# An FFN up-projection computed token-major with moving weight columns, then transposed to channel rows

## The chip, the core and the metric

The kernel runs on one core of a Trainium2 chip. The metric is device time in microseconds of one execution; the kernel before has a median of 1065.43 us over 3 runs (1064.88 to 1066.43).

## What is computed

One decoder layer for 256 tokens of width 2048, in float32. The mixing part (gated convolution, pooling, attention into 256 memory tokens, output projection) stays as it is; the FFN and the final norm follow. With D_FF = 5632:

```python
        h = rmsnorm(x, g_ffn[l])
        u = causal_dwconv(h @ w_up[l], ffn_conv_w[l]) + ffn_conv_b[l]   # 3 taps along the tokens
        gate, val = jnp.split(u, 2, axis=-1)                           # 5632 channels each
        x = x + (jax.nn.silu(gate) * val) @ w_down[l]
    return rmsnorm(x, g_final)
```

## The kernel before

Every float32 operand of a product is split into a high and a low part in the type float32r, and a product is taken as high x high + high x low + low x high. All weights come as one stream of tiles of 1 MB: SyncE's queue loads a tile (`load`, line 118), ScalarE writes its high part (line 129), VectorE the low part by a subtraction (line 130). Loading runs three tiles ahead of use and splitting two; raw, high and low tiles have three buffers each. `next_tile` (line 149) hands out the next tile and issues these steps.

The stages are: memory tokens, the input projection, the mixing work, the output projection (`mm_b`, lines 326 to 344, with transposes of the FFN's input between two of its products, line 719), then the FFN. There the 44 + 44 chunks of 128 gate and value channels go in 22 units of 256 gate and 256 value channels. The units form groups of 8, 7, 5 and 2; the down-projection of a group comes after the next group's first unit, that of the third after all units, and the last one ends the kernel.

An up unit calls `unit_a` for the gates, finishes them, and calls it for the values. `mm_a` (lines 300 to 312) holds weight columns still: for each of 16 chunks k and two chunks of channels, the high weights against the 512 columns of high and low activations of 256 tokens (line 306), then the low weights against the 256 high columns (line 309). The result has channels in rows, in a bank of PSUM whose two halves are still to be added. `up_finish` (line 737) copies one half out on ScalarE (`gather`, line 322), adds the other and multiplies by a row of the tokens' norm factors on VectorE (lines 323, 324). The convolution along the tokens follows: a scaled copy with bias on ScalarE (line 747), two taps on VectorE (line 751), with two zero columns that GpSimd clears as left margin (line 743). Gates go through Silu (line 755); gate times value is split again into the tile `u` (lines 776 to 780).

The down-projection (`down`, lines 782 to 789) goes the other way about: blocks of 128 tokens of `u` stand still and 512 columns of weights move, in two banks by turns. The last group (`down_last`) does the same and then takes 512- or 256-column pieces in one bank (lines 808 to 820).

The first unit differs: its four tiles alternate between gates and values by halves of k, since the second half of the FFN's transposed input is made by 16 transposes after its first tile (line 734). The norm factors are turned into a row by two transposes (`row_of`, line 274).

Tile, the layer that the kernel is written in, puts the instructions of each engine in order between the parts whose order is written out by hand (the head and the last group); it starts from the order of the program and from what is ready. PSUM has 8 banks, handed out one at a time.

Of the kernel before, what the change touches and what calls it, by code (L numbers as in the profile page):

```python
# [15 lines left out]
P = 128  # L16
EPS = 1e-6
HPAD = 6  # buffers for rows with a left margin
WINDOWS = (2, 4, 8, 16)
# Engines whose instructions keep the order of the program in the first and last parts.  # L20
# [4 lines left out]
def kernel(  # L25
# [33 lines left out]
    # Has the activation table loaded before the first data are there.  # L59
    first = cpool.tile([P, 1], F32, name="first")  # L60
    nc.scalar.activation(first, ones[:, 0:1], AF.Copy)
    # Keeps the tensor engine's clock up until the first data are there.
# [8 lines left out]
    # Per-channel vectors, as columns of 128 channels, by transposing rows of 128.  # L71
# [20 lines left out]
    rows = lambda v: v.rearrange("(r c) -> r c", c=P)  # noqa: E731  # L92
# [10 lines left out]
    stream = []  # (source, nk, ncol, pieces)  # L103
# [52 lines left out]
    n_units = NF // 2  # L156
    UNITS = [8, 7, n_units - 17, 2]  # sizes of FFN groups in units of 256 channels
# [20 lines left out]
    # The pool's weights: per pair of groups the three chunks' rows, in the columns of  # L178
    # the output chunks that they reach; wp_at[k] is the first of them.
# [17 lines left out]
    # Chunks of the mix in the order in which they come about.  # L197
# [10 lines left out]
    # A group's down-projection comes after the next group's first unit; that of the  # L208
    # last but one after all units.
    sched = []  # L210
    done = 0
    for gi, (a, n) in enumerate(group_of):
        upto = n_units if gi + 2 >= len(group_of) else a + n + 1
        for u in range(done, upto):
            sched.append(("up", u, [g for g, (b, m) in enumerate(group_of) if b <= u][-1]))
        done = upto
        sched.append(("down", gi, None))
    for what, a, b in sched:
        if what == "up" and a == 0:
            for h in (0, 1):  # L220
                plan_a(w_up, 0, (h,))
                plan_a(w_up, D_UP, (h,))
        elif what == "up":
            plan_a(w_up, a * 256)
            plan_a(w_up, D_UP + a * 256)
        else:
            a0, n = group_of[a]
            for n2 in range(2):
                plan_b(w_down, a0 * 2, n * 2, n2 * 1024, 1024, 2)

# [27 lines left out]
    def rstd_of(ssq, nm):  # L258
        """ssq [P, n] sums of squares -> 1 / sqrt(mean + eps), with a Newton step."""
        n = ssq.shape[1]  # L260
        v = spool.tile([P, n], F32, tag="nv", name=f"v_{nm}")
        r = spool.tile([P, n], F32, tag="nr", name=f"r_{nm}")
        t = spool.tile([P, n], F32, tag="nt", name=f"t_{nm}")
        with tc.high_priority():
            nc.gpsimd.tensor_scalar(v, ssq, 1.0 / D, EPS, op0=ALU.mult, op1=ALU.add)
            nc.scalar.activation(t, v, AF.Sqrt)
            nc.vector.reciprocal(r, t)
            nc.gpsimd.tensor_tensor(t, r, r, op=ALU.mult)
            nc.gpsimd.tensor_tensor(t, t, v, op=ALU.mult)
            nc.gpsimd.tensor_scalar(t, t, -0.5, 1.5, op0=ALU.mult, op1=ALU.add)  # L270
            nc.gpsimd.tensor_tensor(r, r, t, op=ALU.mult)
        return r

    def row_of(r, nm):
        """[P, TB] per-token values -> the same row of S values in every partition."""
        pr = bank(f"prow_{nm}")
        row = cpool.tile([P, S], F32, name=f"row_{nm}")
        with tc.high_priority():
            for tb in range(TB):
                nc.tensor.transpose(  # L280
                    pr[:, tb * P : (tb + 1) * P], r[:, tb : tb + 1].to_broadcast([P, P]), ident
                )
            nc.scalar.activation(row, pr[:, :S], AF.Copy)
        return row
# [35 lines left out]
    def gather(ps, row, o, engine=nc.vector):  # L320
        """(main + corrections) * row -> o [P, S] in SBUF."""
        nc.scalar.activation(o, ps[:, S:], AF.Copy)  # L322
        nc.vector.tensor_tensor(o, ps[:, :S], o, op=ALU.add)
        engine.tensor_tensor(o, o, row, op=ALU.mult)

    def mm_b(ps, wt, actT, ks, tbs, first, last):
        """ps[tb][n] += act[tokens of tb, chunk k] @ w[chunk k, columns of n]."""
# [41 lines left out]
    # The order of the first instructions is that in which the data arrive.  # L369
# [66 lines left out]
    def split_into(o, src, n=S):  # L436
        """float32 [P, n] -> o, its two parts one after the other."""
# [50 lines left out]
    # 1 / (number of tokens averaged) for the first tokens  # L488
# [73 lines left out]
    # The sums run on GpSimd while the next unit's products do; the rest comes after.  # L562
    pending = []

    def pool_sums(ps, i):
# [3 lines left out]
        spans = []  # (first row, last row, group) of this chunk  # L569
# [17 lines left out]
    def pool_means():  # L587
        for i, v, spans, sums in pending:
# [11 lines left out]
            # The convolution's chunks of the mix are free until it comes.  # L600
# [122 lines left out]
    row_2 = None  # L723
    u_tiles = {}

    def up_matmul(u):
        if u:
            return [unit_a(h2T, f"g{u}"), unit_a(h2T, f"v{u}")]
        ps = [[bank(f"pu0_{w}_{mi}") for mi in range(2)] for w in range(2)]
        for h in range(2):  # L730
            for w in range(2):
                mm_a(ps[w], next_tile(), h2T, h * 8, 8, h == 0, h == 1)
                if h == 0 and w == 0:
                    transpose_in(xt, h2T, "g_ffn", range(8, 16), "x2")
        return ps

    def up_finish(ps, u, w):
        """main + corrections, norm, convolution and bias of one half of a unit."""
        outs = []
        for mi in range(2):  # L740
            m = w * NF + u * 2 + mi
            hp = spool.tile([P, S + 2], F32, tag="hpad", name=f"h_{u}_{w}_{mi}", bufs=HPAD)
            nc.gpsimd.memset(hp[:, :2], 0.0)
            gather(ps[mi], row_2, hp[:, 2:])
            t = spool.tile([P, S], F32, tag="w1k", name=f"t_{u}_{w}_{mi}", bufs=6)
            cw = [cvec("ffn_conv_w", j * 2 * NF + m) for j in range(3)]
            nc.scalar.activation(  # L747
                t, hp[:, 2:], AF.Identity, bias=cvec("ffn_conv_b", m), scale=cw[2]
            )
            for s in (1, 0):  # L750
                nc.vector.scalar_tensor_tensor(  # L751
                    t, hp[:, s : s + S], cw[s], t, op0=ALU.mult, op1=ALU.add
# [4 lines left out]
        return outs  # L757

    def up(u, gi):
        nonlocal row_2  # L760
        if gi not in u_tiles:
            u_tiles[gi] = apool.tile([P, 16, 2 * S], F32R, tag="act", name=f"u_{gi}")
        ut = u_tiles[gi]
        base = group_of[gi][0]
        if u == 0:
            ps_g, ps_v = up_matmul(0)
            row_2 = row_of(rstd_sum(ssq4, "x2"), "x2")
            gates = up_finish(ps_g, u, 0)
        else:
            ps_g = unit_a(h2T, f"g{u}")  # L770
            gates = up_finish(ps_g, u, 0)
            ps_v = unit_a(h2T, f"v{u}")
        vals = up_finish(ps_v, u, 1)
        for mi in range(2):
            c = (u - base) * 2 + mi
            nc.vector.tensor_tensor(gates[mi], gates[mi], vals[mi], op=ALU.mult)
            nc.scalar.activation(ut[:, c, :S], gates[mi], AF.Copy)
            nc.vector.tensor_tensor(
                ut[:, c, S:], gates[mi], ut[:, c, :S].bitcast(F32), op=ALU.subtract
            )  # L780

    def down(gi):
        ut = u_tiles[gi]
        nk = group_of[gi][1] * 2
        for n2 in range(2):
            ps = [[bank(f"pd_{gi}_{n2}_{tb}_{n}") for n in range(2)] for tb in range(TB)]
            for i in range(nk // 2):
                mm_b(ps, next_tile(), ut, (2 * i, 2 * i + 1), range(TB), i == 0, i == nk // 2 - 1)
            add_in(ps, n2 * 2, range(TB), f"d{gi}")

    # The last group goes by token blocks and column pieces, each followed by its share
    # of the final norm, so that little is left after the last product.
    def down_last(gi):
        ut = u_tiles[gi]
        nk = group_of[gi][1] * 2
        gfin = wpool.tile([P, D], F32, tag="raw", name="gfin")
        nc.sync.dma_start(gfin, g_final[None, :].to_broadcast([P, D]))
        nc.scalar.activation(gfin, gfin, AF.Copy, scale=-0.5)  # goes with -2 / sqrt
# [28 lines left out]
        def partial(tb):  # L827
            """The mean square + eps, but for the last piece."""
# [4 lines left out]
        def rstd_last(tb):  # L833
            """-2 / sqrt(mean square + eps), with a Newton step."""
# [20 lines left out]
        with tc.manual_schedule(engines=IN_ORDER):  # L855
# [3 lines left out]
            for tb in range(TB):  # L859
                for p in range(2):  # L860
                    add(ps[tb][p], tb, p)
                    square(tb, p)
                    if tb == 0 and p == 0:
                        # has the square root's table loaded
# [23 lines left out]
    for what, a, b in sched:  # L888
        if what == "up":
            up(a, b)  # L890
# [35 lines left out]
```

## Time and profile before

| | |
|---|---|
| median of 3 runs | 1065.43 us (1064.88 to 1066.43) |
| span of the profiled execution | 1064.7 us |
| TensorE products busy | 1054.7 us (99%), 5632 |
| weight loads on TensorE busy | 907.2 us (85%) |
| VectorE busy | 703.6 us (66%) |
| ScalarE busy | 529.0 us (50%) |
| GpSimd busy | 43.1 us (4%) |
| DMA | 202.01 MB, mean 190 GB/s |

Busy times are of one profiled execution. A product's record runs past the start of the next one, so busy time of TensorE doesn't tell how near it is to its peak; the distance between starts does. In the rows, PE is TensorE, PEld its weight loads, DVE VectorE, ACT ScalarE and POOL GpSimd; L306 is line 306; `pa_g` and `pa_v` are the banks of the gates and values, `pd` and `pl` those of the down-projection, `po` of the output projection, `pt_x` those of the transposes.

### The profile page before, as it was taken

How to read it: one execution, taken by the hardware profiler on the slowest of the kernel's cores; microseconds unless marked ns; L12 is line 12 of the kernel's file. 1: busy time of each engine (PE TensorE's matmuls, PEld its weight loads, DVE VectorE, ACT ScalarE, POOL GpSimd, SP SyncE). 2: the span in 40 equal slices, each digit the busy share in tenths (PEclk: the TensorE clock that was granted, in tenths of full speed). 3: DMA queues.
4: the chain of work that ended last, by engine and by line, in shares of the span. 5: the costliest groups of instructions: out<-in, count | busy, mean ns of one | idle time of the engine just before them, and what ended most of it. 6: DMA issues, size and time to landing. Idle time of an engine off the chain costs nothing.

```text
span 1064.7 us, 14249 instructions
## 1 busy us (share of the span) xinstructions
PE 1054.7 (99%) x5632; PEld 907.2 (85%) x5632; DVE 703.6 (66%) x920; ACT 529.0 (50%) x683; POOL 43.1 (4%) x163
## 2 busy tenths in 40 slices
PE   9999999999999999999999999999999999999996
PEld 8888898888888888888888888888888888888885
DVE  5677786764556777777744467777754477777655
ACT  5965454443446655555533344554533345555343
POOL 0023500000000000000000000000000000000000
PEclk9999999999999999999999999999999999999998
DMA  9765465455555556555555555655555555654552
GB/s 316 243 224 172 143 206 189 161 195 183 186 185 174 184 196 198 188 181 185 198 198 198 196 171 187 198 185 175 195 198 197 191 174 190 198 177 178 198 198 80
DMA packets 147342, 202.01 MB, mean 190 GB/s; under 512 B 3619, under 2 KB 125771, under 8 KB 147147
## 3 DMA queue, kind: packets, MB, share of 16 engines
q1 hardware_dynamic: 147242, 201.09, 55.8%
q8 instruction: 44, 0.72, 0.3%
q14 instruction: 24, 0.19, 0.0%
q10 hardware_dynamic: 32, 0.01, 0.0%
HBM read 198.99 MB, written 2.10 MB: 189 GB/s over the span
## 4 chain that ended last, share of the span: by engine, by line
PE 98%; DVE 1%; ACT 0%; issue 0%; DVEq 0%
PE pa_v L306 15%; PE pa_g L306 15%; PE pa_g L309 7%; PE pa_v L309 7%; PE pd L338 7%; PE pd L344 7%; PE pd L341 7%; PE po L338 3%; PE po L341 3%; PE po L344 3%; PE pa_cc L306 2%; PE pa_cx L306 2%; PE pa_cb L306 2%; PE pa_pv L306 2%; PE pk L395 2%; PE pa_q L306 1%
## 5 line engine op out<-in xcount | busy, mean ns | idle before, releaser
L130 DVE TENSOR_TENSOR lo<-raw,hi 128x2048 fp32r<-128x2048 f32 (+2 forms) x196 | 425.5, 2172 | 271.6 <-ACT hi L129 270.6
L129 ACT ACTIVATE hi<-raw 128x2048 fp32r<-128x2048 f32 (+2 forms) x196 | 355.9, 1818 | 255.8 <-PE pd L344 98.4
L306 PE MATMUL pa_v<-h2T,hi 128*128 128x512 f32 x672 | 236.7, 396 | 0.0
L306 PE MATMUL pa_g<-h2T,hi 128*128 128x512 f32 x672 | 236.7, 396 | 0.0
L309 PE MATMUL pa_g<-h2T,lo 128*128 128x256 f32 x672 | 188.5, 281 | 0.0
L309 PE MATMUL pa_v<-h2T,lo 128*128 128x256 f32 x672 | 188.5, 281 | 0.0
L306 PEld LDWEIGHTS pa_v<-h2T,hi 128*128 128x128 f32 x672 | 126.0, 188 | 30.0
L306 PEld LDWEIGHTS pa_g<-h2T,hi 128*128 128x128 f32 x672 | 126.0, 188 | 30.0
L309 PEld LDWEIGHTS pa_g<-h2T,lo 128*128 128x128 f32 x672 | 127.0, 189 | 0.1
L309 PEld LDWEIGHTS pa_v<-h2T,lo 128*128 128x128 f32 x672 | 127.0, 189 | 0.0
L338 PE MATMUL pd<-hi,u 128*128 128x512 f32 x320 | 98.6, 389 | 0.0
L341 PE MATMUL pd<-lo,u 128*128 128x512 f32 x320 | 98.5, 389 | 0.0
L344 PE MATMUL pd<-hi,u 128*128 128x512 f32 x320 | 98.5, 389 | 0.0
L751 DVE SCALAR_TENSOR_TENSOR t<-h,cols,t 128x256 f32<-128x256 f32 x176 | 79.1, 480 | 2.2 <-ACT t L747 1.4
L755 ACT ACTIVATE t<-t 128x256 f32<-128x256 f32 x44 | 18.3, 418 | 107.0 <-DVE t L751 107.0
L341 PEld LDWEIGHTS pd<-lo,u 128*128 128x128 f32 x320 | 60.1, 188 | 12.6
L344 PEld LDWEIGHTS pd<-hi,u 128*128 128x128 f32 x320 | 60.1, 188 | 12.4
L338 PEld LDWEIGHTS pd<-hi,u 128*128 128x128 f32 x320 | 59.9, 188 | 12.4
L747 ACT ACTIVATE t<-h,cols 128x256 f32<-128x256 f32 x88 | 49.8, 593 | 0.0
L322 ACT ACTIVATE h<-pa_g 128x256 f32<-128x256 f32 x42 | 16.0, 380 | 61.3 <-PE pa_g L309 61.3
L338 PE MATMUL po<-hi,mixT 128*128 128x512 f32 x128 | 39.6, 391 | 0.0
L341 PE MATMUL po<-lo,mixT 128*128 128x512 f32 x128 | 39.5, 389 | 0.0
(207 smaller groups left out, 1280.9 us busy)
## 6 DMA issues: line engine op xcount, KB each, us to landing
raw<-in_w_up_dram SPq DMA_DIRECT2D x88, 1024.0 KB, 5.0
raw<-in_w_down_dram SPq DMA_DIRECT2D x44, 1024.0 KB, 4.9
raw<-in_w_in_dram SPq DMA_DIRECT2D x28, 1024.0 KB, 4.9
raw<-in_w_out_dram SPq DMA_DIRECT2D x16, 1024.0 KB, 4.9
raw<-in_w_kv_dram SPq DMA_DIRECT2D x4, 1024.0 KB, 5.2
raw<-in_w_kv_dram SPq DMA_DIRECT2D x6, 512.0 KB, 8.3
memt<-in_mem_dram SPq DMA_DIRECT2D x8, 256.0 KB, 7.7
xt<-in_x_dram SPq DMA_DIRECT2D x4, 512.0 KB, 6.7
```

The costliest lines, as they stand in the source:

```text
L129: nc.scalar.activation(hi[:, s, :], raw[:, s, :], AF.Copy)
L130: nc.vector.tensor_tensor(lo[:, s, :], raw[:, s, :], hi[:, s, :].bitcast(F32), op=ALU.subtract)
L306: nc.tensor.matmul(ps[mi], hi[:, kk, c], actT[:, k, :], start=first and kk == 0, stop=False)
L309: nc.tensor.matmul(ps[mi][:, S:], lo[:, kk, c], actT[:, k, :S], start=False, stop=last and kk == nk - 1,)
L322: nc.scalar.activation(o, ps[:, S:], AF.Copy)
L338: nc.tensor.matmul(ps[tb][n], ah, hi[:, kk, c], start=f, stop=False)
L341: nc.tensor.matmul(ps[tb][n], ah, lo[:, kk, c], start=False, stop=False)
L344: nc.tensor.matmul(ps[tb][n], al, hi[:, kk, c], start=False, stop=l)
L395: nc.tensor.matmul(psk[mi], wt[0][:, j, c], mT[:, k, :], start=k == 0, stop=False)
L747: nc.scalar.activation(t, hp[:, 2:], AF.Identity, bias=cvec("ffn_conv_b", m), scale=cw[2])
L751: nc.vector.scalar_tensor_tensor(t, hp[:, s : s + S], cw[s], t, op0=ALU.mult, op1=ALU.add)
L755: nc.scalar.activation(t, t, AF.Silu)
```

## The change

The up-projection turns round. A unit now has 512 gate and 512 value channels, so there are 11, in groups of 4, 4, 2 and 1. For each half (gates or values) four tiles of 4 chunks k by 512 columns are used. A block of 128 tokens of the activations stands still and the 512 weight columns move: per k and token block three products, all into one bank, so that a half unit fills two banks, one for each token block, with tokens in rows. ScalarE copies each bank out into a tile `z`, with the norm factor as its per-row scale. Eight transposes on TensorE turn the two `z` tiles into channel rows, in two further banks with two chunks each. The scaled copy with bias and the two taps read these banks in PSUM; the taps leave out the first one or two tokens in place of reading zero columns. Silu, the product and the split into `u` stay, by four chunks at a time.

The transposes and all that follows are put off: they are issued after the first token block of the next half's first tile, or after the first tile of a down-projection if that is next. The first unit still alternates between gates and values, by pairs of tiles, and 16 transposes of the FFN's input come after its first tile. The norm factors are used as columns, so the two transposes that made them a row go, as do the sums of two halves, the products with that row and the clears on GpSimd.

The diff, without the comments that it removes and with unchanged or repeated parts left out:

```diff
-    n_units = NF // 2
-    UNITS = [8, 7, n_units - 17, 2]  # sizes of FFN groups in units of 256 channels
+    n_units = NF // 4
+    UNITS = [4, 4, n_units - 9, 1]
+    def part_of(u, b):
+        return (b // 2 % 2, b % 2 + b // 4 * 2) if u == 0 else (b // 4, b % 4)
     for what, a, b in sched:
-        if what == "up" and a == 0:
-            for h in (0, 1):
-                plan_a(w_up, 0, (h,))
-                plan_a(w_up, D_UP, (h,))
-        elif what == "up":
-            plan_a(w_up, a * 256)
-            plan_a(w_up, D_UP + a * 256)
+        if what == "up":
+            for b in range(8):
+                w, q = part_of(a, b)
+                plan_b(w_up, 4 * q, 4, w * D_UP + a * 512, 512, 4)
-    def up_matmul(u):
...
-    def up_finish(ps, u, w):
-        for mi in range(2):
-            hp = spool.tile([P, S + 2], F32, tag="hpad", name=f"h_{u}_{w}_{mi}", bufs=HPAD)
-            nc.gpsimd.memset(hp[:, :2], 0.0)
-            gather(ps[mi], row_2, hp[:, 2:])
...
+    up_ps, up_gates, todo, r_2 = {}, {}, [], []
+    def up(u, b):
+        w, q = part_of(u, b)
+        if q == 0:
+            up_ps[w] = [bank(f"pu{u}_{w}_{tb}") for tb in range(TB)]
+        ps = up_ps[w]
+        hi, lo = next_tile()
+        for tb in range(TB):
+            for kk in range(4):
+                k = 4 * q + kk
+                ah = h2T[:, k, tb * P : (tb + 1) * P]
+                al = h2T[:, k, S + tb * P : S + (tb + 1) * P]
+                for n, (x_, y_) in enumerate(((ah, hi), (ah, lo), (al, hi))):
+                    nc.tensor.matmul(
+                        ps[tb], x_, y_[:, kk, :],
+                        start=k == 0 and n == 0, stop=k == KC - 1 and n == 2,
+                    )
+            if tb == 0 and todo:
+                todo.pop(0)()
+        if u == 0 and b == 0:
+            for k in range(8, 16, 2):
+                split_turned(turn_pair(xt, k, "x2"), h2T, "g_ffn", k)
+            r_2.append(rstd_sum(ssq4, "x2"))
+        if q < 3:
+            return
+        z = []
+        for tb in range(TB):
+            z.append(spool.tile([P, 512], F32, tag="w2k", name=f"z_{u}_{w}_{tb}"))
+            nc.scalar.activation(z[tb], ps[tb], AF.Copy, scale=r_2[0][:, tb : tb + 1])
+        todo.append(lambda: up_finish(u, w, z))
+
+    def up_finish(u, w, z):
+        pt = []
+        for c in range(4):
+            if c % 2 == 0:
+                pt.append(bank(f"pz{u}_{w}_{c}"))
+            for tb in range(TB):
+                o = c % 2 * S + tb * P
+                nc.tensor.transpose(pt[-1][:, o : o + P], z[tb][:, c * P : (c + 1) * P], ident)
+        for c in range(4):
+            v = pt[c // 2][:, c % 2 * S : (c % 2 + 1) * S]
+            m = w * NF + u * 4 + c
...
+            nc.scalar.activation(t, v, AF.Identity, bias=cvec("ffn_conv_b", m), scale=cw[2])
+            for s in (1, 2):
                 nc.vector.scalar_tensor_tensor(
-                    t, hp[:, s : s + S], cw[s], t, op0=ALU.mult, op1=ALU.add
+                    t[:, s:], v[:, : S - s], cw[2 - s], t[:, s:], op0=ALU.mult, op1=ALU.add
                 )
...
+        for c in range(4):
+            nc.vector.tensor_tensor(gates[c], gates[c], outs[c], op=ALU.mult)
+            split_into(u_tiles[gi][:, (u - group_of[gi][0]) * 4 + c, :], gates[c])
     def down(gi):
...
                 mm_b(ps, next_tile(), ut, (2 * i, 2 * i + 1), range(TB), i == 0, i == nk // 2 - 1)
+                while todo:
+                    todo.pop(0)()
```

## Rows read from the trace of the kernel before

**Rows 1.** The page: busy time by engine; granted clock in slices; the chain

```profile
PE 1054.7 (99%) x5632; PEld 907.2 (85%) x5632; DVE 703.6 (66%) x920; ACT 529.0 (50%) x683; POOL 43.1 (4%) x163
...
PEclk9999999999999999999999999999999999999998
...
PE 98%; DVE 1%; ACT 0%; issue 0%; DVEq 0%
```

**Rows 2.** Waits of TensorE in the whole span: total us, times, longest us

```profile
PE warm L67 <- DVE ones L58: 1.0, 1, 1.0
PE pk L395 <- DVE mT L249: 0.3, 1, 0.3
```

**Rows 3.** Windows: stretch, us, busy of PE, PEld, DVE, ACT, POOL; clock, DMA

```profile
320.35:522.10 201.75, 201.75 (x1171) 178.04 (x1170) 150.84 (x217) 113.41 (x157) 4.28 (x38) 1.00 0.57 188
522.10:609.18 87.08, 87.08 (x386) 72.08 (x385) 44.42 (x34) 33.16 (x23) 0.30 (x3) 1.00 0.56 193
609.18:767.47 158.29, 158.29 (x898) 137.19 (x897) 114.03 (x159) 81.46 (x106) 2.61 (x26) 1.00 0.56 187
843.65:979.32 135.67, 135.67 (x769) 117.69 (x768) 97.32 (x135) 69.50 (x90) 1.81 (x18) 1.00 0.56 187
```

**Rows 4.** TensorE timeline (start, us, instruction): half unit, its first and the next

```profile
499.92 0.39 PE L306 MATMUL pa_g<-h2T,hi 128*128 128x512 f32 x1
...
511.01 0.39 PE L306 MATMUL pa_v<-h2T,hi 128*128 128x512 f32 x1
```

**Rows 5.** Timeline of TensorE: twelve 512-column products into one bank, first and next

```profile
1044.61 0.39 PE L817 MATMUL pl<-hi,u 128*128 128x512 f32 x1
...
1047.33 0.28 PE L817 MATMUL pl<-hi,u 128*128 128x256 f32 x1
```

**Rows 6.** Timeline of TensorE: two groups of eight transposes between products

```profile
291.32 1.03 PE L237 MATMUL pt_x<-ident,xt 128*128 128x128 f32 x8
292.11 0.70 PE L338 MATMUL po<-hi,mixT 128*128 128x512 f32 x2
...
297.66 1.04 PE L237 MATMUL pt_x<-ident,xt 128*128 128x128 f32 x8
```

**Rows 7.** Groups by line and shape: transposes, weight loads (busy, mean | idle)

```profile
L237 PE MATMUL pt_x<-ident,xt 128*128 128x128 f32 x64 | 8.8, 273 | 0.0
L306 PEld LDWEIGHTS pa_v<-h2T,hi 128*128 128x128 f32 x672 | 126.0, 188 | 30.0
```

**Rows 8.** Groups by line and shape: VectorE, ScalarE in the up-projection

```profile
L130 DVE TENSOR_TENSOR lo<-raw,hi 128x2048 fp32r<-128x2048 f32 x175 | 401.4, 2294 | 264.8 <-ACT hi L129 264.5
L324 DVE TENSOR_TENSOR h<-h,row_x 128x256 f32<-128x256 f32 x88 | 35.4, 421 | 0.8
L751 DVE SCALAR_TENSOR_TENSOR t<-h,cols,t 128x256 f32<-128x256 f32 x176 | 79.1, 480 | 2.2 <-ACT t L747 1.4
L249 DVE SCALAR_TENSOR_TENSOR h2T<-pt_x,cols,h2T 128x256 fp32r<-128x256 f32 x16 | 6.5, 476 | 0.0
L479 ACT ACTIVATE misc<-pv,r_mem 128x512 fp32r<-128x512 f32 x2 | 1.3, 675 | 0.0
L747 ACT ACTIVATE t<-h,cols 128x256 f32<-128x256 f32 x88 | 49.8, 593 | 0.0
```

**Rows 9.** Timeline of ScalarE at the ends of two half units

```profile
500.24 0.64 ACT L322 ACTIVATE h<-pa_v 128x256 f32<-128x256 f32 x2
510.92 0.39 ACT L322 ACTIVATE h<-pa_g 128x256 f32<-128x256 f32 x1 [2.79 <-PE pa_g L309]
511.20 1.91 ACT L129 ACTIVATE hi<-raw 128x2048 fp32r<-128x2048 f32 x1
513.50 0.38 ACT L322 ACTIVATE h<-pa_g 128x256 f32<-128x256 f32 x1
```

More of the change, by code (lines that the diff above doesn't have):

```diff
@@ L153, in next_tile @@
         return split.pop(i)
-    n_units = NF // 2
-    UNITS = [8, 7, n_units - 17, 2]
+    n_units = NF // 4
+    UNITS = [4, 4, n_units - 9, 1]
+    assert NF % 4 == 0
     D_UP = DFF
@@ L214 @@
         for u in range(done, upto):
-            sched.append(("up", u, [g for g, (b, m) in enumerate(group_of) if b <= u][-1]))
+            sched.append(("up", u, None))
         done = upto
@@ L228 @@
             for n2 in range(2):
-                plan_b(w_down, a0 * 2, n * 2, n2 * 1024, 1024, 2)
+                plan_b(w_down, a0 * 4, n * 4, n2 * 1024, 1024, 2)
     def turn_pair(xt, k, nm):
@@ L720 @@
         add_in(ps, n2 * 2, range(TB), f"o{n2}", ssq4)
-    row_2 = None
     u_tiles = {}
-    def up_matmul(u):
[L727 to L735, printed above, removed]
@@ L737, in up_finish @@
-    def up_finish(ps, u, w):
-        outs = []
-        for mi in range(2):
-            m = w * NF + u * 2 + mi
-            hp = spool.tile([P, S + 2], F32, tag="hpad", name=f"h_{u}_{w}_{mi}", bufs=HPAD)
-            nc.gpsimd.memset(hp[:, :2], 0.0)
-            gather(ps[mi], row_2, hp[:, 2:])
-            t = spool.tile([P, S], F32, tag="w1k", name=f"t_{u}_{w}_{mi}", bufs=6)
+    up_ps, up_gates, todo, r_2 = {}, {}, [], []
[28 more added lines that the diff above has]
+        todo.append(lambda: up_finish(u, w, z))
@@ new lines, in up_finish @@
+    def up_finish(u, w, z):
[6 more added lines that the diff above has]
+                nc.tensor.transpose(pt[-1][:, o : o + P], z[tb][:, c * P : (c + 1) * P], ident)
+        outs = []
+        for c in range(4):
+            v = pt[c // 2][:, c % 2 * S : (c % 2 + 1) * S]
+            m = w * NF + u * 4 + c
+            tag, n, bufs = ("w1k", S, 6) if w else ("hpad", PAD + S, HPAD)
+            t = spool.tile([P, n], F32, tag=tag, name=f"t_{u}_{w}_{c}", bufs=bufs)[:, :S]
@@ L746, in up_finish @@
             cw = [cvec("ffn_conv_w", j * 2 * NF + m) for j in range(3)]
[L747 to L750, printed above, removed]
+            nc.scalar.activation(t, v, AF.Identity, bias=cvec("ffn_conv_b", m), scale=cw[2])
+            for s in (1, 2):
                 nc.vector.scalar_tensor_tensor(
-                    t, hp[:, s : s + S], cw[s], t, op0=ALU.mult, op1=ALU.add
+                    t[:, s:], v[:, : S - s], cw[2 - s], t[:, s:], op0=ALU.mult, op1=ALU.add
@@ L756, in up_finish @@
             outs.append(t)
-        return outs
-    def up(u, gi):
-        nonlocal row_2
+        if w == 0:
+            up_gates[u] = outs
+            return
+        gates = up_gates.pop(u)
+        gi = [g for g, (a, n) in enumerate(group_of) if a <= u][-1]
         if gi not in u_tiles:
             u_tiles[gi] = apool.tile([P, 16, 2 * S], F32R, tag="act", name=f"u_{gi}")
[L763 to L780, printed above, removed]
+        for c in range(4):
+            nc.vector.tensor_tensor(gates[c], gates[c], outs[c], op=ALU.mult)
+            split_into(u_tiles[gi][:, (u - group_of[gi][0]) * 4 + c, :], gates[c])
     def down(gi):
         ut = u_tiles[gi]
-        nk = group_of[gi][1] * 2
+        nk = group_of[gi][1] * 4
         for n2 in range(2):
@@ L794, in down_last @@
         ut = u_tiles[gi]
-        nk = group_of[gi][1] * 2
+        nk = group_of[gi][1] * 4
         gfin = wpool.tile([P, D], F32, tag="raw", name="gfin")
@@ L889 @@
         if what == "up":
-            up(a, b)
+            for b in range(8):
+                up(a, b)
         elif a < len(group_of) - 1:
```

## The prediction, made before the changed kernel was run

> **What bounds the kernel now.** I read the page first. Its busy line has TensorE at 99% of the span, VectorE at 66% and ScalarE at 50%, and the chain that ended last lies on TensorE for 98% [rows 1]. The clock line shows the higher of the two levels, 2.4 GHz, in all 40 slices. So any TensorE time that is taken away shortens the kernel, and any that is added lengthens it, as long as nothing else becomes late. Second, the waits: in the whole span TensorE waits twice, 1.3 us in all, both near the start [rows 2]. The up-projection holds no stall that a change could remove. Third, the windows cut at the first product of each up and down stage [rows 3]: three up stages of 201.75, 158.29 and 135.67 us, 495.7 together, with granted clock 1.00, VectorE at about 72 to 75% and the DMA engines at 0.56 to 0.57. The down stage beside them has the same clock and DMA load. Busy time of TensorE cannot price a product, because products overlap in the record: a row says 0.39 us, but the next one starts earlier. The price is the distance from one start to the next, so I use stretches divided by counts.
>
> **The change, part by part: the products.** Before, one 128-channel chunk and one k take two products: the high part of the weights against 512 columns, and the low part against 256. There are 88 chunks and 16 k, so 1408 pairs, 2816 products. After, one unit, half, k and token block takes three products of 512 columns: 11 x 2 x 16 x 2 x 3 = 2112. The columns are equal, 1408 x 768 = 2112 x 512, and only the time per column can differ. The pair: one half unit of 32 pairs lasts from 499.92 to 511.01 [rows 4], 347 ns a pair. The second and third up stages hold 7 and 6 units of 64 pairs and nothing else on TensorE, 158.29/448 and 135.67/384 [rows 3], 353 ns a pair. Over all up stages: 495.7 us less 16 transposes of the FFN's input and 2 of its norm at 0.11 us (below), 2.0 us, leaves 493.7 us. The new product has its nearest relative in the down stage: activations standing, 512 weight columns moving, 87.08 us for 384 products [rows 3], 226.8 ns. There two banks alternate, whereas the new loop writes one bank three times in a row. The last group of the kernel has just that form, twelve products into one bank from 1044.61 to 1047.33 [rows 5], 226.7 ns. I take 226.7: 2112 x 226.7 = 478.8 us, **14.9 us less**.
>
> **The transposes.** Each of the 22 half units is turned by 4 chunks x 2 token blocks = 8 transposes, 176 in all. They are the same operation as those of the FFN's input, which stand between products in the output projection. There eight transposes and 24 products repeat after 297.66 - 291.32 = 6.34 us [rows 6]; less 24 x 0.2267 = 5.44 that is 0.90 us for a group, including the few products after it that run slightly late. 22 x 0.90 = **19.8 us more**. They are not hidden, since TensorE has no idle time to take them [rows 2]. The two transposes of the norm row go: 0.2 us less.
>
> The record gives one transpose 273 ns [rows 7], more than twice the 0.11 us that a group costs per transpose. The Trainium skill, "TensorE: Matmul & The Clock Gate", Part 4, states a figure much like that row, about 275 ns for a transpose in a kernel; I estimate from it 176 x 275 = 48 us in place of 19.8. The spacing of rows 6 speaks against it, and I keep it as a rival.
>
> **What leaves TensorE alone.** The sum of the two halves and the norm's product on VectorE go (88 additions and 88 products of 0.42 us, the second of them in [rows 8]), about 74 us. The taps' 176 instructions stay at 0.48 us; that they read PSUM costs nothing by the nearest row, 0.476 us for the same kind of instruction out of PSUM [rows 8]. So VectorE per new unit, by 8 weight splits, 16 taps and 8 instructions of 0.42: 18.4 + 7.7 + 3.4 = 29.5 us of some 45, 65%. On ScalarE the 88 copies out of PSUM become 44 of twice the width, 0.675 us by the nearest row [rows 8], about equal in sum. The 88 small clears on GpSimd go; nobody waits for that engine in this stage. The weight tiles keep their megabyte each and their number, 88, and read 2 KB rows in place of 1 KB ones; the DMA share of 0.57 [rows 3] leaves room. The groups become 8, 8, 4 and 2 old units in place of 8, 7, 5 and 2: the same down products, and the last group is as large as it was. All of this is covered by TensorE's own 44 us per unit; without the cover, the taps would cost up to 8 us a unit.
>
> **The wait that the change adds.** The transposes wait for two copies on ScalarE, the second of which can start only when the half unit's last product has ended. Behind them in TensorE's queue stand the other 12 products of the next tile. The cover is the 12 products that come first, 12 x 0.2267 = 2.72 us. The copies need about 0.7 us once ScalarE is free; before the change both copies at the end of a half unit begin 0.3 us after it and take 0.64 [rows 9]. From below I take nothing, as no stall exists to be removed. From above: at the end of the other half, the second copy (513.50) stands behind a weight split and a tap, and ends at 513.88, 2.9 us after the half unit [rows 9]. With that order, and copies twice as long, the transposes wait 0.2 to 0.5 us each time, 4 to 11 us in all. I put that order down to the split, which may start one product before the bank is full: the last product of the half unit reads the low weights only. The new loop ends on a product that reads the high weights, so the copy and the split come free together and the copy stands first in the program. I take nothing. In the down stages the cover is a whole tile, 5.4 us.
>
> **Sum.** -14.9 + 19.8 - 0.2 = +4.7 us. The profiled span is 1064.67 us, so 1069.4; the median of the runs lies 0.76 above that span, which gives **1070.1 us**, 0.44% slower. About 0.2%, 2.1 us, is what a measurement of this kernel can tell from no change.
>
> **The rivals.** (a) *The transposes wait for their copies*, the order of rows 9 in all 22 half units: 1074 to 1081 us. The order in the trace speaks for it; the 2.72 us of cover and the absence of any such wait so far [rows 2] speak against. Chance 0.18.
> (b) *Products settle late.* Transposes disturb the spacing of the products behind them; the pair itself runs at 347 or 353 ns for whole stages [rows 3, 4], so the spacing can stay in a slower pattern. A 512-column product at two thirds of the 353 ns pair would take 235.5 ns, 2112 x 8.8 = 18.6 us more, 1089; half of it, 1079. Against: the 24 products between the groups of rows 6 are back in step within 0.03 us. Chance 0.05.
> (c) *Faster: the second of two neighbouring products with the same standing block costs only its columns.* Each (token block, k) has one such pair, 704 of them. 512 columns at 2.4 GHz are 213.3 ns, 13.4 below 226.7: 9.4 us less, 1060.7. It decides from 6.7 ns per product on, where it pays for the 4.7 us. Against it stands the down stage, where one block serves up to four products in a row and the mean is still 226.8. Chance 0.04.
> A rule would carry that side further. One 128 x 128 weight load is recorded at 188 ns [rows 7], and 704 fewer are issued; if loads stood between products, 132 us would go and the kernel would take 933 us. The Trainium skill, "TensorE: Matmul & The Clock Gate", Part 3, says that a load overlaps a running product only if it goes to other rows of the array, which none here does. Two loads, 376 ns, are longer than the 347 ns pair that holds them [rows 4, 7], so they must overlap. Chance 0.02.
> (d) *The transposes cost their recorded 273 ns*, 48 us: 1098. Chance 0.02.
> (e) *A wash*: a group of eight costs only the 0.79 us from its first transpose to the next product [rows 6], with none late behind it. That is 17.4 us in all and +2.3 in the sum, 1067.7, at the edge of 0.2%; the runs' spread of 0.8 us decides. Chance 0.07.
>
> **How the numbers follow.** The forecast has 0.62, and its own range is 1068.5 to 1072 (group of eight at 0.87 to 0.95 us, spread of the runs). The range leaves out (c), (d), the loads' rule, the upper end of (a), the upper part of (b) and half of (e): 1067 to 1079. Slower: forecast, (a), (b), (d), 0.87. Same: (e), 0.07. Faster: (c) and the loads' rule, 0.06.
>
> **What would show each step.** After the change, the up stages should hold 512-column products 226.7 ns apart; 22 groups of eight transposes, each adding about 0.9 us; no waits of TensorE on ScalarE; VectorE near 59% of the span (703.6 - 74 us); granted clock 1.00 throughout. A wait of a transpose on a copy points to (a), a spacing of 230 to 236 ns to (b), of under 220 in every third place to (c). I am wrong if the transposes stand somewhere where TensorE is idle, or if TensorE waits at all in the up stages.

## The result: 1069.6 us, 0.44% slower

The changed kernel has a median of 1069.63 us, against 1065.31 us for the kernel before: ratio 1.0044, interval 1.003 to 1.0057. The forecast was 1070.1 us and slower; the time lies 0.5 us from it and inside its range.

The profile's page of the changed kernel: busy time and count by engine, the granted clock, the chain by engine and the first lines of the chain by line.

```profile
PE 1057.3 (99%) x5102; PEld 888.2 (83%) x5102; DVE 642.8 (60%) x744; ACT 530.5 (50%) x638; POOL 34.2 (3%) x75
...
PEclk9999999999999999999999999999999999999999
...
PE 99%; DVE 0%; ACT 0%; DVEq 0%; issue 0%
PE pu L743 45%; PE pd L344 7%; PE pd L347 7%; PE pd L341 7%; PE po L344 3%; PE po L341 3%; PE po L347 3%; PE pa_cx L309 2%; PE pa_cc L309 2%; PE pa_pv L309 2%; PE pa_cb L309 2%; PE pz L769 2%; PE pk L398 1%; PE pa_q L309 1%; PE pa_cb L312 1%; PE pa_cc L312 1%
```

Against [rows 1], nothing changed hands: TensorE is still the chain, at the same clock level. The new name in the chain is `pz`, the transposes, with 2% of the span, some 20 us; VectorE fell from 66% to 60%, and the span did not notice. All waits of TensorE:

```profile
PE warm L67 <- DVE ones L58: 1.1, 1, 1.1
PE pk L398 <- DVE mT L252: 0.9, 1, 0.9
```

As in [rows 2], both are at the very start. No product and no transpose of the FFN waited for anything.

Windows of the changed kernel, cut at the first product of each up and down stage (stretch, us, busy of PE, PEld, DVE, ACT, POOL; clock, DMA share, GB/s):

```profile
318.50:546.24 227.74, 227.74 (x1050) 189.37 (x1048) 138.10 (x157) 124.68 (x150) 0.97 (x5) 1.00 0.56 185
546.24:634.20 87.96, 87.96 (x393) 72.90 (x392) 46.12 (x38) 34.30 (x25) 0.00 (x0) 1.00 0.55 191
634.20:814.77 180.57, 180.57 (x825) 149.97 (x824) 106.79 (x115) 92.93 (x103) 0.00 (x0) 1.00 0.56 187
814.77:902.74 87.97, 87.97 (x394) 72.90 (x392) 46.13 (x38) 34.30 (x25) 0.00 (x0) 1.00 0.55 191
902.74:992.55 89.81, 89.81 (x409) 74.57 (x408) 51.05 (x51) 44.61 (x47) 0.00 (x0) 1.00 0.56 187
992.55:1037.00 44.45, 44.45 (x201) 36.87 (x200) 27.88 (x30) 20.68 (x18) 0.00 (x0) 1.00 0.53 190
```

The six stretches come to 718.5 us. The same part before, from 320.35 to the last group's first product at 1033.73, took 713.4 us (four of its six stretches are [rows 3]). So the FFN up to the last group became 5.1 us longer; the forecast had 4.7. The span grew by 3.2 us only, since the part ahead of the FFN was 1.85 us shorter in this profiled execution. In the execution of the kernel before that was profiled, the first products ran at about half the speed. Its first group of four 512-column products, then that after the change (start, us, instruction; the next product starts at 8.62 and at 7.46, so they stand 0.46 and 0.25 us apart):

```profile
6.78 2.04 PE L395 MATMUL pk<-mT,hi 128*128 128x512 f32 x4 [0.26 <-DVE mT L249]
```

```profile
6.45 1.17 PE L398 MATMUL pk<-mT,hi 128*128 128x512 f32 x4 [0.87 <-DVE mT L252]
```

That spacing fits the lower of the two clock levels; the windows of these first microseconds give a granted clock of 1.00 in both, so the level is read from the spacing alone. That part is the same code in both, and its length changes from profile to profile: in two experiments below that leave it alone, group sizes and the first disturbance, the first up product starts at 319.47 and at 318.68. In the experiments, most single runs of the kernel before lie near 1064.7 us and some near 1066.4, about as far apart as the two lengths of that part. It belongs to no step of the change, and the stage itself is the better measure of it: 5.1 us.

One half unit in steady state (TensorE, start, us, instruction), from one group of transposes to the next:

```profile
390.16 1.04 PE L769 MATMUL pz<-ident,z 128*128 128x128 f32 x8
...
412.85 1.04 PE L769 MATMUL pz<-ident,z 128*128 128x128 f32 x8
```

It is 22.69 us, of which 96 products at 226.7 ns are 21.76 and the group of eight 0.93.

### The profile page after: what moved, and what is told of

Same layout as the page of the kernel before. It is cut to its first block, busy times and chain, and to the rows that moved or that the text cites. A ratio compares the mean times of both kernels' runs of the same rounds, so it can differ in the third digit from the quotient of the medians.

```text
span 1067.9 us, 12641 instructions
## 1 busy us (share of the span) xinstructions
PE 1057.3 (99%) x5102; PEld 888.2 (83%) x5102; DVE 642.8 (60%) x744; ACT 530.5 (50%) x638; POOL 34.2 (3%) x75
## 4 chain that ended last, share of the span: by engine, by line
PE 99%; DVE 0%; ACT 0%; DVEq 0%; issue 0%
PE pu L743 45%; PE pd L344 7%; PE pd L347 7%; PE pd L341 7%; PE po L344 3%; PE po L341 3%; PE po L347 3%; PE pa_cx L309 2%; PE pa_cc L309 2%; PE pa_pv L309 2%; PE pa_cb L309 2%; PE pz L769 2%; PE pk L398 1%; PE pa_q L309 1%; PE pa_cb L312 1%; PE pa_cc L312 1%
## 5 line engine op out<-in xcount | busy, mean ns | idle before, releaser
L743 PE MATMUL pu<-hi,h2T 128*128 128x512 f32 x1408 | 439.8, 391 | 0.0
L743 PEld LDWEIGHTS pu<-hi,h2T 128*128 128x128 f32 x1408 | 264.3, 188 | 54.7
L743 PE MATMUL pu<-lo,h2T 128*128 128x512 f32 x704 | 273.8, 389 | 0.0
L743 PEld LDWEIGHTS pu<-lo,h2T 128*128 128x128 f32 x704 | 132.3, 188 | 26.9
L779 DVE SCALAR_TENSOR_TENSOR t<-pz,cols,t 128x255 f32<-128x255 f32 (+1 forms) x176 | 80.0, 479 | 15.3 <-ACT t L777 14.2
L777 ACT ACTIVATE t<-pz,cols 128x256 f32<-128x256 f32 x88 | 46.8, 557 | 37.2 <-DVE t L779 24.7
L341 PE MATMUL po<-hi,mixT 128*128 128x512 f32 x128 | 39.6, 391 | 0.0
L347 PE MATMUL po<-hi,mixT 128*128 128x512 f32 x128 | 39.4, 389 | 0.0
L309 PE MATMUL pa_cb<-hT,hi 128*128 128x512 f32 x96 | 34.2, 399 | 0.0
L309 PE MATMUL pa_cx<-hT,hi 128*128 128x512 f32 x96 | 34.1, 399 | 0.0
L309 PE MATMUL pa_cc<-hT,hi 128*128 128x512 f32 x96 | 34.0, 399 | 0.0
```

What stands on the lines that cost most here:

```text
L309: nc.tensor.matmul(ps[mi], hi[:, kk, c], actT[:, k, :], start=first and kk == 0, stop=False)
L341: nc.tensor.matmul(ps[tb][n], ah, hi[:, kk, c], start=f, stop=False)
L347: nc.tensor.matmul(ps[tb][n], al, hi[:, kk, c], start=False, stop=l)
L743: nc.tensor.matmul(ps[tb], x_, y_[:, kk, :], start=k == 0 and n == 0, stop=k == KC - 1 and n == 2,)
L777: nc.scalar.activation(t, v, AF.Identity, bias=cvec("ffn_conv_b", m), scale=cw[2])
L779: nc.vector.scalar_tensor_tensor(t[:, s:], v[:, : S - s], cw[2 - s], t[:, s:], op0=ALU.mult, op1=ALU.add)
```

## Experiments

Times are compared with the kernel before, run on the same chip beside each: 1064.73 us for no transposes, transposes twice, group sizes and the first disturbance, 1064.70 for the last disturbance, 1064.68 for the others.

**No transposes.** The copies stay, the scaled copy and the taps read `z` in SBUF, and the two `pz` banks go. The kernel leaves out the turning, so its output is not the layer's.

```diff
-                nc.tensor.transpose(pt[-1][:, o : o + P], z[tb][:, c * P : (c + 1) * P], ident)
...
-            v = pt[c // 2][:, c % 2 * S : (c % 2 + 1) * S]
+            v = z[c // 2][:, c % 2 * S : (c % 2 + 1) * S]
```

> The changed kernel without its 176 transposes; the copies and taps read the z tiles in SBUF as they stand, so channels and tokens are not put in their rows. If the products save 15 us and the transposes cost 0.93 us per group of eight, wholly on TensorE's path, 22 x 0.93 = 20.5 us go: 1069.6 - 20.5 = 1049 us, which is 16 us below the kernel before. If the transposes were partly hidden, less goes: 1055 to 1069. If they cost the 273 ns of their records, 48 us go: 1022.

Measured: 1049.70 us, 15.0 below the kernel before (ratio 0.9860, interval 0.9844 to 0.9877). The forecast had 14.9 us less for the products and 0.2 for the norm row. The second up stage, now products alone (window, as above):

```profile
625.11:799.19 174.08, 174.08 (x770) 144.19 (x768) 105.71 (x118) 95.53 (x105) 0.00 (x0) 1.00 0.56 193
```

174.08 us for 4 units x 2 halves x 96 = 768 products is 226.7 ns each. So the two large terms of the sum stand on their own, and did not come out right only by cancelling: with the transposes back, 19.3 us return by the two differences of medians (15.0 + 4.3), and 20.1 with the 5.1 us of the stage.

**Transposes twice.**

```diff
-                nc.tensor.transpose(pt[-1][:, o : o + P], z[tb][:, c * P : (c + 1) * P], ident)
+                for _ in range(2):
+                    nc.tensor.transpose(
+                        pt[-1][:, o : o + P], z[tb][:, c * P : (c + 1) * P], ident
+                    )
```

> The changed kernel with each of the 176 transposes issued twice in a row to the same place. If a transpose costs its distance of 0.109 us on the path, 176 x 0.109 = 19.2 us more: 1088.8 us. If it costs its record of 273 ns: 1118. If part of a group is a fixed cost of going from products to transposes and back, less than 19 us is added here while leaving the groups out takes more than that away.

Measured: 1089.07 us, 24.3 above the kernel before, 20 above the change. Two neighbouring groups on TensorE:

```profile
392.01 1.91 PE L770 MATMUL pz<-ident,z 128*128 128x128 f32 x16
...
415.57 1.91 PE L770 MATMUL pz<-ident,z 128*128 128x128 f32 x16
```

The half unit grew from 22.69 to 23.56 us: 0.87 for eight more, 0.109 each. The remaining 0.06 of the 0.93 is what it costs to go from products to transposes and back. The price of 273 ns, which the records show, is refuted: it would have made 1118 us here. The Trainium skill, "TensorE: Matmul & The Clock Gate", Part 4, gives about 275 ns for a 128x128 transpose (of bf16) in a kernel. That is near the record here, and not what a transpose in a row costs on the path, 109 ns; the measurement decides.

**Group sizes alone**, in the kernel before.

```diff
-    UNITS = [8, 7, n_units - 17, 2]
+    UNITS = [8, 8, n_units - 18, 2]
```

> The kernel before with the sizes of its FFN groups alone changed, 8, 8, 4 and 2 units in place of 8, 7, 5 and 2, as the changed kernel has them. By the forecast nothing: 1065.3 us within 1. If the later down-projection or the smaller third group left something uncovered, TensorE shows a wait in the FFN and the time grows by its length.

Measured: 1064.78 us, ratio 1.0002 (0.9993 to 1.0012). The regrouping is free.

**Narrow products.** The changed kernel with half the columns a product.

```diff
-                    nc.tensor.matmul(
-                        ps[tb], x_, y_[:, kk, :],
-                        start=k == 0 and n == 0, stop=k == KC - 1 and n == 2,
-                    )
+                    for c in (0, 256):
+                        nc.tensor.matmul(
+                            ps[tb][:, c : c + 256], x_, y_[:, kk, c : c + 256],
+                            start=k == 0 and n == 0 and c == 0,
+                            stop=k == KC - 1 and n == 2 and c == 256,
+                        )
```

> The changed kernel with each 512-column product of the up-projection cut into two of 256 columns with the same standing block: the same columns, twice the weight loads. If what the pair of before lost is a weight load that a 256-column product does not wholly cover, the products take 120 ns, as the 256-column pieces of the last group did: 4224 x 120 = 507 against 479 us, 1098 us. If time goes by columns alone, 1070.

Measured: 1096.62 us, 31.9 above the kernel before, 27.6 above the change (31.9 less 4.3); 4224 x 120 less 479 makes 28.1. A half unit, again from one group to the next:

```profile
394.23 1.04 PE L771 MATMUL pz<-ident,z 128*128 128x128 f32 x8
...
418.13 0.38 PE L771 MATMUL pz<-ident,z 128*128 128x128 f32 x2
```

23.90 us less 0.93, over 192 products: 119.6 ns for 256 columns, where half of 226.7 is 113.3; away from the transposes the starts are 120 ns apart. (The second row shows two transposes because its window ends there.) So time does not go by columns alone. The two distances give an estimate of how it goes: 256 columns more make 226.7 - 120 = 106.7 ns, so a product has some 13.3 ns beside its columns, a wide one as much as a narrow one. A pair of 512 and 256 would then take 3 x 106.7 + 2 x 13.3 = 346.7 ns, and the first up stage of before has 347 [rows 4]. The expectation's reason, a weight load that 256 columns do not wholly cover, is not shown by this: the 512 columns would have to leave as much of it uncovered. Every product here has a load of its own, so whether the 13.3 ns belong to the product or to its load stays open.

**Wide low products**, in the up-projection of the kernel before.

```diff
+    h2T = None
...
+                wide = actT is h2T
                 nc.tensor.matmul(
-                    ps[mi][:, S:], lo[:, kk, c], actT[:, k, :S],
+                    ps[mi] if wide else ps[mi][:, S:], lo[:, kk, c],
+                    actT[:, k, :] if wide else actT[:, k, :S],
```

> The kernel before with the low weights of the up-projection taken against all 512 columns, so that its pair is two products of 512 columns; weights still stand and activations still move (the low times low part is added, which the kernel leaves out otherwise). If the width of the product decides, they run 226.7 ns apart: 1408 x (453.4 - 350.7) = 145 us more, 1210 us. If the orientation decides and the 512-column product keeps the 233 ns that it has in the pair, 467: 1229 us.

Measured: 1209.42 us, 144.7 above the kernel before. One half unit of 64 products:

```profile
393.37 0.39 PE L306 MATMUL pa_v<-h2T,hi 128*128 128x512 f32 x1
...
407.88 0.39 PE L306 MATMUL pa_g<-h2T,hi 128*128 128x512 f32 x1
```

14.51 us, 226.7 ns a product, with weights standing. This is the cleanest of the nine: the orientation gives nothing. What the change gained on its products, it gained because they are all 512 columns wide. The old pair takes 347 or 353 ns where its 768 columns in wide products would take 340. By the estimate above 6.7 of these 7 to 13 ns come from its being two products for one and a half; the other 6, in the stages at 353, are looked at below.

**No cover for the copies.** The change with the put-off work at the head of the next tile.

```diff
         hi, lo = next_tile()
+        if todo:
+            todo.pop(0)()
...
-            if tb == 0 and todo:
-                todo.pop(0)()
```

> The changed kernel with the transposes of a half unit issued at the start of the next half's first tile, ahead of its 12 products of the first token block and not behind them. If those 12 products are the cover for the copies on ScalarE, TensorE waits for the second copy, about 0.9 us (0.69 for the copy and what lies around it), in the half units that another half follows, 19 of 22: 17 us, 1087. If the order of instructions is rearranged around the wait, or the copies are done anyway, 1069.6.

Measured: 1071.50 us, ratio 1.0068 (1.0052 to 1.0084), 2.6 us more than the change. The first theory, a wait of 0.9 us per half unit, fell; the second, a rearranged order, holds, though it is not free. TensorE at one half unit's end, then ScalarE there:

```profile
389.62 0.38 PE L769 MATMUL pz<-ident,z 128*128 128x128 f32 x2
389.76 0.47 PE L745 MATMUL pu<-hi,h2T 128*128 128x512 f32 x1
390.07 0.39 PE L745 MATMUL pu<-lo,h2T 128*128 128x512 f32 x1
390.31 0.40 PE L745 MATMUL pu<-hi,h2T 128*128 128x512 f32 x1
390.56 0.88 PE L769 MATMUL pz<-ident,z 128*128 128x128 f32 x6
...
412.41 0.38 PE L769 MATMUL pz<-ident,z 128*128 128x128 f32 x2
```

```profile
387.10 0.69 ACT L758 ACTIVATE z<-pu,r_x 128x512 f32<-128x512 f32 x1 [0.76 <-PE pu L745]
389.82 0.69 ACT L758 ACTIVATE z<-pu,r_x 128x512 f32<-128x512 f32 x1 [2.04 <-PE pu L745]
```

In the order of instructions that Tile chose, two transposes come first, then three products, and the other six transposes when the second copy has ended (390.51). The half unit is 22.79 us in place of 22.69: being broken in two costs 0.10, or 2 us over the kernel. The 12 products of cover are worth that much, and not the 17 us of a true wait.

**A disturbance ahead of the up stages.** The pairs of the kernel before run at 347 ns in the first up stage and at 353 in the other two [rows 3, 4]. Two transposes of the identity, whose result nobody reads, ahead of the units 9 and 16:

```diff
+            if u in (9, 16):
+                pt = bank(f"nudge_{u}")
+                for i in range(2):
+                    nc.tensor.transpose(pt[:, i * P : (i + 1) * P], ident, ident)
             ps_g = unit_a(h2T, f"g{u}")
```

> The kernel before with two idle transposes ahead of the first up unit after the first and after the second down-projection; the pairs of those two up stages (13 units) ran at 353 ns where those of the first stage, which has transposes in it, ran at 347. If the spacing of pairs is a pattern that the work just ahead sets and that then lasts for the whole stage, the 26 half units go to 347: 26 x 32 x 6.7 ns = 5.6 us less, 0.3 more for the transposes, 1060 us. If the spacing comes from the stage itself (buffers, other engines), 1065.6.

Measured: 1065.19 us, ratio 1.0000 (0.9991 to 1.0010). A half unit in the second stage:

```profile
619.05 0.40 PE L306 MATMUL pa_v<-h2T,hi 128*128 128x512 f32 x1
...
630.36 0.40 PE L306 MATMUL pa_g<-h2T,hi 128*128 128x512 f32 x1
```

Still 11.31 us, 353 ns a pair, and the third stage did not change either (136.0 us with its two transposes, 135.7 before); the first theory fell. Next, the same transposes after the first 16 pairs of the gates of those units:

```diff
             mm_a(ps, next_tile(), actT, h * 8, 8, h == 0, h == 1)
+            if h == 0 and nm in ("g9", "g16"):
+                pt = bank(f"nudge_{nm}")
+                for i in range(2):
+                    nc.tensor.transpose(pt[:, i * P : (i + 1) * P], ident, ident)
```

> The kernel before with two idle transposes after the first tile (16 pairs) of the gates of the first unit behind the first and the second down-projection. In the first up stage transposes that stood between pairs were followed by a spacing of 347 ns, while two transposes right behind a down-projection were followed by 353. If the place between pairs decides, 25 half units go to 347: 25 x 32 x 6.7 ns = 5.4 us less, 0.5 more for the transposes: 1060 us. If it does not, 1065.5.

Measured: 1062.31 us, ratio 0.9981 (0.9972 to 0.9991), less than half of what was expected. A half unit of the second stage, and one of the third:

```profile
618.82 0.39 PE L306 MATMUL pa_v<-h2T,hi 128*128 128x512 f32 x1
...
629.91 0.39 PE L306 MATMUL pa_g<-h2T,hi 128*128 128x512 f32 x1
...
862.06 0.40 PE L306 MATMUL pa_g<-h2T,hi 128*128 128x512 f32 x1
...
873.36 0.40 PE L306 MATMUL pa_v<-h2T,hi 128*128 128x512 f32 x1
```

The second stage went to 11.09 us (347 ns) and stayed there for 13 half units; the third stayed at 11.30 (353 ns), with the same transposes in the same place. Last, three more places in the third stage (`"g16", "v16", "g17", "v17"`):

> The kernel before with idle pairs of transposes between the two tiles of the gates of unit 9 and of the gates and values of units 16 and 17, five places. With two such places the second up stage went from 353 to 347 ns a pair and the third stayed at 353. If each disturbance between pairs may bring either pattern, and the 347 ns one lasts once it is reached, the third stage changes at one of its four places: up to 2.4 us less than with two places, 0.7 more for three further pairs of transposes, 1060.6 to 1063.0 us. If the third stage cannot leave the pattern, 1063.0.

Measured: 1062.90 us, ratio 0.9981 (0.9972 to 0.9990): the third stage did not move, and the extra transposes cost their price. The stage keeps a pattern that a disturbance can change in one place and not in another; what decides it stays open. With two places this is the fastest kernel of the study that computes the layer, 2.4 us below the kernel before and some 7 below the changed one (the latter by the two ratios, 0.9981 and 1.0044), and it rests on an effect that is not understood.

## Why the prediction was right

**The products: right.** Removed 493.7 us, added 2112 x 226.7 = 478.8. The up stage without transposes shows 226.7 ns and a gain of 15.0 us in all. The choice that mattered was to price the new product by the distance between starts, in [rows 5] or in the down stage (226.8), and not by the record's 0.39 us. (The clock line of [rows 1] reads 9 in 39 slices and 8 in the last, at the very end of the kernel, and not the top in all 40; no term hangs on it.)

**Why they are cheaper: not asked for by the sum, and known in part.** The forecast only read two spacings. The wide and narrow kernels show that the width of the products decides, and fit a price of some 13.3 ns for each product beside its columns. There are 704 products fewer, 9.4 us. The remaining 5.5 of the 14.9 us are the slower rhythm of the second and third up stages, 832 pairs x 6.6 ns, which the new loop does not have. That part is no property of the old form: two idle transposes took away 2.4 us net in one of the stages. The forecast counted it as one, which was right for the kernel as it stood. The rule of Part 3 of the Trainium skill's "TensorE: Matmul & The Clock Gate", by which such loads would stand between products, stays refuted: with 704 loads fewer 15 us went, not 132, and in the narrow kernel 119.6 ns hold a product with a load that is itself recorded at about 190.

**The transposes: right, 3% small.** 0.93 us for a group in place of 0.90, 20.4 us in place of 19.8. Those 0.6 us, less 0.1 or 0.2 of rounding in the other terms, are the difference between the 5.1 measured in the stage and 4.7. The group of [rows 6] was read from a place where two banks alternate behind it. In the new loop the step from the last transpose to the next product is the same, 0.79 us after the first transpose, but the products behind it fall back into step a little later: they lose 0.13 us in place of 0.11. The first stands 0.31 us from the next in both places; then follow nine distances of 224 to 236 ns in the new loop and six in the old place, until the 226.7 are back.

**The wait: right in its result, and the order is the one given.** The forecast said that the copy comes free together with the weight split and stands first. ScalarE at the end of a half unit of the changed kernel:

```profile
407.60 0.69 ACT L758 ACTIVATE z<-pu,r_x 128x512 f32<-128x512 f32 x1 [0.80 <-PE pu L743]
410.32 0.69 ACT L758 ACTIVATE z<-pu,r_x 128x512 f32<-128x512 f32 x1 [2.03 <-PE pu L743]
410.90 1.91 ACT L129 ACTIVATE hi<-raw 128x2048 fp32r<-128x2048 f32 x1
```

The second copy ends at 411.01 and the split comes behind it (their records overlap by 0.1 us); the transposes follow at 412.85. The slack is 1.84 us. Rival (a) would have needed the order of [rows 9], which did not come. That the split could not have started earlier, the reason that the forecast gave, follows from the program and is not shown by these rows. The experiment without cover adds that a missing cover need not make a wait, because Tile may put TensorE's instructions in another order. The rival's price of 4 to 11 us took that order as given by the program; whether it would have changed under the order of [rows 9] no run shows. (What the forecast calls a tap there, at 513.01, is the scaled copy of line 747.)

**The other engines: harmless, as said, with one term mis-sized.** VectorE was to lose 74 us of busy time and lost 61 (703.6 to 642.8). Count times mean overstates it: instructions that follow each other closely overlap in the record, so that the sums and norm products that left held 71 us and not 74, and the taps, with the same mean, now hold 82 us where they held 79 [rows 8], because fewer of them overlap. Of the other 7 us, 2.4 are the products of gate and value and the subtractions of the split, which also overlap less, and nearly 5 are overlaps between different groups: all groups of VectorE add up to 28.2 us more than its busy time before, and to 23.3 more after. Nothing waits for any of this. The taps out of PSUM cost what was taken from the nearest row (two groups by shape, busy, mean ns | idle before and what ended it):

```profile
L777 ACT ACTIVATE t<-pz,cols 128x256 f32<-128x256 f32 x88 | 46.8, 557 | 37.2 <-DVE t L779 24.7 <-PE pz L769 12.5
L779 DVE SCALAR_TENSOR_TENSOR t<-pz,cols,t 128x255 f32<-128x255 f32 x88 | 41.7, 480 | 14.2 <-ACT t L777 14.2
```

The regrouping, the wider rows of the weights (DMA share still 0.56) and the clears were free, as said.

**The rivals.** (b) and (c) both fell with 226.7 ns throughout, but for the ten products behind each group, which are in its price; (d) with the doubled transposes; (e) had 2.3 us in its sum and the stage shows 5.1, since the group costs 0.93 and not 0.79.

**The last step to 1070.1: close, and partly by luck.** The forecast put the median 0.76 us above the profiled span. But every run on record takes about 1.8 us longer than its own span, so the profiled execution, 1064.67, belongs to the run of 1066.43 us, one with the long first part. The step did no harm, since it only puts the 4.7 us on the median of three runs, 1065.43. That base is 0.7 us above the usual 1064.7, and 4.7 is 0.4 below the 5.1 of the stage; the two misses offset each other.

## What to carry to other kernels

Where one engine is the whole chain, a change of form is decided by two prices on that engine, and both can be read off the kernel before, as distances from start to start in a stretch that already has the new form; the recorded duration of one product or transpose is the wrong number for this. Turning operands round does not make a product cheaper here; fewer and wider products do, by some 13 ns for each product saved, and 8 transposes of 0.109 us for every 96 products ate the gain and 0.4% of the time on top. Before paying for a rearrangement, ask whether the width can be had without the part that has to be undone.

## What the runs showed of the hardware that was not expected

Products in a regular sequence keep a rhythm. The same pairs run at 347 or at 353 ns for hundreds of products, and two transposes worth 0.3 us shifted one stage to its end, 2.4 us in all, in one place out of seven tried. Averaged over a stage, all of the 6 ns lie between the start of the wide product and that of the narrow one, 236 or 230 ns; from the narrow to the next wide one it is 117 in both. What sets the rhythm stays open.

ScalarE's scaled copy out of a `pz` bank waited 24.7 us in all, 11 times, once a unit, for VectorE's taps (row L777 above), though both only read. The two chunks of a bank were worked on one after the other. The Trainium skill, "PSUM — Partial Sum Buffer", "PSUM bank collisions raise a hardware error", says that two engines must not be in one bank and the same partitions at the same time, reads included; the waits agree with an order kept for that reason. The kernel without transposes bears it out: there the same copies and taps read SBUF, and none of the 88 copies waited for VectorE (by shape, busy, mean ns | idle before):

```profile
L770 ACT ACTIVATE t<-z,cols 128x256 f32<-128x256 f32 x88 | 47.9, 593 | 0.7
```

Here the half unit of 22 us covers the wait. In a kernel bound by ScalarE or VectorE, two chunks to a bank may cost time; no run here shows one.
